# Gate and up products with the tokens held still and the weights streamed; ten of eleven gate chunks from seven Strassen block products

## The chip, the core and the metric

The kernel runs on one core of one Trainium2 chip, as one launch. The metric is the device time of that launch in microseconds (us). Three runs of the kernel before took 1958.15, 1959.32 and 1959.55 us, so its median is 1959.32 us.

## The reference

One decoder block for 256 tokens of width 2048, all in float32:

```
x = layer_norm(2**0.25 * x + 0.5 * swiglu(x, ffn1_w_gate, ffn1_w_up, ffn1_w_down))
x = layer_norm(2**0.25 * x + hybrid_mixer(x))          # attention heads and an RG-LRU branch
x = layer_norm(2**0.25 * x + 0.5 * swiglu(x, ffn2_w_gate, ffn2_w_up, ffn2_w_down))
x = x + sigmoid(x @ w_ple_gate) * (p @ w_ple_proj)

swiglu(x, g, u, d) = (silu(x @ g) * (x @ u)) @ d       # g, u: 2048 x 5632, d: 5632 x 2048
```

The change concerns `swiglu`, which runs twice. Its three weights make up most of what the kernel reads: 528 of the 684 entries of 512 KB belong to them.

## The kernel before

**Numbers in two parts.** TensorE multiplies in a 32-bit format that keeps 12 bits of a factor. So every factor is split in two parts, hi and lo: ScalarE (ACT) writes the rounded hi part (line 86 for weights, line 60 for activations), VectorE (DVE) subtracts it from the original and writes lo (lines 92 and 61). A product is then the sum of three: hi·hi, hi·lo and lo·hi. The tokens are kept transposed in `xT` (16 blocks of 128 input channels, hi and lo).

**The plan.** `make_plan` lists the weights in the order in which the products take them, in entries of 256 rows by 512 columns (512 KB). Each entry is loaded into one of 5 buffers `raw` by SyncE's queue, split into one of 9 slots `hi` and `lo`, and used. `advance` prepares entries up to 7 ahead (`AHEAD`) while a slot is free (`SLOTS`); a slot is free again when the products that read it are done. The order within each engine is the order in which this program writes the instructions.

**The feed-forward stage.** `swiglu` takes the 5632 inner channels in 11 chunks of 512. For each chunk it forms the gate (8 entries) and the up product (8 entries) with `group_a`: a 128x128 block of weights is held in TensorE and the 256 tokens stream past it. For each weight block there are two matmuls: hi of the weights against hi and lo of the tokens (512 columns), and lo of the weights against hi of the tokens (256 columns). The result has the inner channels on the partitions. `evac_a` adds the two halves of a bank (lines 307 and 308), the sigmoid follows (line 412), and the activation is split (lines 60 and 61). Then `down` multiplies the activation of the **previous** chunk by its 8 entries of the third weight, activation held still and weights streamed (three matmuls of 512 columns per block), and adds into `acc` (line 315). So a chunk's activation has two whole products, some 45 us, to become ready before it is used.

**The rest.** The mixer uses `group_a` for 6 groups (`channels`) and `group_b`, which holds tokens still and streams weights, for 5; small pieces of the RG-LRU and the attention are put between entries by `tick`. At the first product after a layer norm (`boundary`) the second half of the tokens is still being transposed, so the products take the two halves of the tokens one after the other.

Of the kernel before, what the change touches and what calls it, by code (L numbers as in the profile page):

```python
# [17 lines left out]
NCH = FF // 512  # L18
QW, KVW, LRU = 1536, 512, 1536
C_X = QW + 2 * KVW  # L20
C_Y = C_X + LRU
HOOKS = (4, 5, 6, 7)
# [9 lines left out]
AHEAD = 7  # L32
SLOTS = 9
# [3 lines left out]
class Block:  # L37
# [26 lines left out]
    def load(self, q):  # L64
        e = self.plan[q]
        if e.get("load"):
            e["load"]()
        e["raw"] = self.tile(self.wraw, [P, 2, 512], F32, "raw")
        for k in e["parts"]:
            self.nc.sync.dma_start(e["raw"][:, k, :], e["src"][:, k, :])  # L70

    def prepare_hi(self, q):
        while self.loaded < min(len(self.plan), q + 4):
            self.load(self.loaded)
            self.loaded += 1
        e = self.plan[q]
        if e.get("split"):
            e["split"]()
        if e["work"]:
            e["hi"], e["lo"] = self.wide_r((P, 2, 512)), self.wide_r((P, 2, 512))  # L80
        else:
            e["hi"] = self.tile(self.whi, [P, 2, 512], F32R, "hi")
            e["lo"] = self.tile(self.wlo, [P, 2, 512], F32R, "lo")
            self.live += 1
        for k in e["parts"]:
            self.nc.scalar.copy(e["hi"][:, k, :], e["raw"][:, k, :])  # L86

    def prepare_lo(self, q):
        e = self.plan[q]
        eng = self.nc.gpsimd if e["pool"] else self.nc.vector  # L90
        for k in e["parts"]:
            eng.tensor_tensor(e["lo"][:, k, :], e["raw"][:, k, :], e["hi"][:, k, :].bitcast(F32), op=ALU.subtract)  # L92
# [9 lines left out]
    def advance_lo(self, end):  # L102
        while self.ready_lo < end:
            self.prepare_lo(self.ready_lo)
            self.ready_lo += 1
# [23 lines left out]
    def tick(self):  # L129
        self.ticks += 1  # L130
        if self.ticks % 2:
            self.tick_lru()
        for queue in (self.att_q, self.gate_q, self.res_q):
            self.step(queue)
# [7 lines left out]
    def make_plan(self):  # L142
        i = self.i
        plan = self.plan = []

        def add(w, r0, c0, n=1, **kw):
            for j in range(n):
                plan.append({"src": self.rows2(w, r0 + 256 * j, c0), "work": False, "pool": False,
                             "parts": [slice(0, 2)], **kw})

        def ffn(name):
            g, u, d = (i[f"{name}_w_{v}"] for v in ("gate", "up", "down"))
            for c in range(NCH):
                add(g, 0, c * 512, 8)
                add(u, 0, c * 512, 8)
                if c:
                    down(d, (c - 1) * 512)
            down(d, (NCH - 1) * 512)

        def down(w, r0):  # L160
            for n in range(4):
                add(w, r0, n * 512, 2)

        w, wo = i["w_in"], i["w_out"]
        ffn("ffn1")
        for j in range(8):
            plan[j]["load"] = lambda j=j: self.load_x(j)
            plan[j]["split"] = lambda j=j: self.split_x(j)
            plan[16 + j]["load"] = lambda j=j: self.load_acc(j)
        plan[0]["parts"] = [slice(0, 1), slice(1, 2)]  # L170
        v0 = len(plan)
        add(w, 0, QW + KVW, 8)
        for g in range(3):
            add(w, 0, C_X + g * 512, 8)
        for h in range(4):
            add(w, 0, h * 512, 8)
        for g in range(3):
            add(w, 0, C_Y + g * 512, 8)
            down(wo, g * 512)
        down(wo, 3 * 512)  # L180
        f0 = len(plan)
        ffn("ffn2")
        p0 = len(plan)
        for n in range(4):
            add(i["w_ple_proj"], 0, n * 512)
        for n in range(4):
            add(i["w_ple_gate"], 0, n * 512, 8)
        for q in (v0, f0, p0):
            for e in plan[q:q + 3]:
                e["work"] = e["pool"] = True  # L190
        plan[p0]["load"], plan[p0]["split"] = self.load_p, self.split_p
        self.xraw = {}
        self.limit = len(plan)
        self.loaded = self.ready = self.ready_lo = self.taken = self.live = 0
        self.ticks = 0
        self.lru_q, self.att_q, self.gate_q, self.res_q = [], [], [], []

    def rows2(self, w, r0, c0):
        return w[r0:r0 + 256, c0:c0 + 512].rearrange("(k p) c -> p k c", p=P)

# [33 lines left out]
    def group_a(self, on_block, boundary=False):  # L234
        banks = [self.bank() for _ in range(4)]
        if not boundary:
            for j in range(8):
                e = self.take()
                self.tokens_a(e, j, banks, slice(0, 256), True, on_block)
                self.done(e)  # L240
                self.tick()
            return
        es = []
        self.limit = self.taken + 8
        for j in range(8):
            es.append(self.take())
            self.tokens_a(es[j], j, banks, slice(0, P), True)
            if j == 1:
                self.advance_lo(self.ready)
            if j in HOOKS:  # L250
                self.ln_transpose(1, HOOKS.index(j))
        self.limit = len(self.plan)
        self.res_q.append(self.ln_residual())
        for j in range(8):
            self.tokens_a(es[j], j, banks, slice(P, 256), False, on_block)
            self.done(es[j])
            self.tick()
# [69 lines left out]

    def down(self, acts, first):
        for n in range(4):
            es = [self.take(), self.take()]  # L330
            for t in range(2):
                self.down_mm(acts, es, t, n, first)
                self.tick()
            for e in es:
                self.done(e)
# [66 lines left out]
    def swiglu(self, boundary):  # L402
        nc = self.nc
        pend = None
        for c in range(NCH):
            gate = []

            def on_gate(b, bank):
                g = self.narrow()
                self.evac_a(bank, g)  # L410
                s = self.narrow()
                nc.scalar.activation(s, g, AF.Sigmoid)  # L412
                nc.vector.tensor_tensor(g, g, s, op=ALU.mult)  # L413
                gate.append(g)

            self.group_a(on_gate, boundary and c == 0)
            if c == 1 and not boundary:
                self.res_q.append(self.tables())
            ah, al = self.wide_r(), self.wide_r()

            def on_up(b, bank):
                u = self.narrow()
                self.evac_a(bank, u)
                nc.vector.scalar_tensor_tensor(u, gate[b], 0.5, u, op0=ALU.mult, op1=ALU.mult)  # L424
                self.split(ah[:, b, :], al[:, b, :], u)

            self.group_a(on_up)
            if pend is not None:
                self.down(pend, c == 1)
            pend = (ah, al)  # L430
        self.down_last(pend)

# [299 lines left out]
    def build(self):  # L732
        tc = self.tc
        with (
            tc.tile_pool(name="const", bufs=1) as self.const,
            tc.tile_pool(name="small", bufs=2) as self.small,
            tc.tile_pool(name="wraw", bufs=5) as self.wraw,
            tc.tile_pool(name="whi", bufs=SLOTS) as self.whi,
            tc.tile_pool(name="wlo", bufs=SLOTS) as self.wlo,
            tc.tile_pool(name="work", bufs=12) as self.work,  # L740
            tc.tile_pool(name="work1", bufs=6) as self.work1,
# [58 lines left out]
```

## Time and profile before

| | |
|---|---|
| median of three runs | 1959.32 us |
| profiled execution, first to last instruction (span) | 1958.6 us |
| TensorE matmuls busy | 1946.0 us, 99% |
| TensorE weight loads busy | 1665.9 us, 85% |
| VectorE busy | 1293.7 us, 66% |
| ScalarE busy | 962.3 us, 49% |
| GpSimd busy | 151.2 us, 8% |
| DMA queue of the weights, share of 16 engines | 58.4% |
| mean DMA rate | 192 GB/s |

The profiled execution is one of the same program; its span stands 0.7 us under the median of the runs. Busy times are unions: a matmul that starts while the one before it drains counts once. So the step from one matmul's start to the next is the time that a matmul takes in a row of them, and not the duration shown beside it, which includes the drain.

### The profile page before, as it was taken

How to read it: one execution, taken by the hardware profiler on the slowest of the kernel's cores; microseconds unless marked ns; L12 is line 12 of the kernel's file. 1: busy time of each engine (PE TensorE's matmuls, PEld its weight loads, DVE VectorE, ACT ScalarE, POOL GpSimd, SP SyncE). 2: the span in 40 equal slices, each digit the busy share in tenths (PEclk: the TensorE clock that was granted, in tenths of full speed). 3: DMA queues.
4: the chain of work that ended last, by engine and by line, in shares of the span. 5: the costliest groups of instructions: out<-in, count | busy, mean ns of one | idle time of the engine just before them, and what ended most of it. 6: DMA issues, size and time to landing. Idle time of an engine off the chain costs nothing.

```text
span 1958.6 us, 26578 instructions
## 1 busy us (share of the span) xinstructions
PE 1946.0 (99%) x10244; PEld 1665.9 (85%) x10244; DVE 1293.7 (66%) x1679; ACT 962.3 (49%) x1330; POOL 151.2 (8%) x93
## 2 busy tenths in 40 slices
PE   8999999999999999999999999999999999999999
PEld 7888888888888888888888898888888888888787
DVE  6667565656665666778677786566556656565875
ACT  6544444444444446656754545444444444444552
POOL 0000000000000012301100250000000000000151
PEclk9999999999999999999999999999999999999999
DMA  9666565556655665655456466656565656655563
GB/s 315 206 210 201 166 218 190 174 171 215 205 176 177 193 205 183 226 163 171 141 193 194 150 207 222 195 172 219 168 214 173 195 169 217 193 173 172 178 223 132
DMA packets 195007, 375.27 MB, mean 192 GB/s; under 512 B 11953, under 2 KB 14657, under 8 KB 194881
## 3 DMA queue, kind: packets, MB, share of 16 engines
q1 hardware_dynamic: 193856, 370.42, 58.4%
q0 software_dynamic: 1024, 3.16, 0.5%
q8 instruction: 80, 1.31, 0.3%
q14 instruction: 47, 0.38, 0.1%
HBM read 371.43 MB, written 2.10 MB: 191 GB/s over the span
## 4 chain that ended last, share of the span: by engine, by line
PE 99%; DVE 1%; DMA 0%; issue 0%; ACT 0%; SPq 0%; POOL 0%; DVEq 0%
PE mm L203 98%; PE mm L380 1%; DVE w L61 0%; DMA raw<-in_ffn_w_gate_dram 0%; DVE lo L92 0%; PE mm L586 0%; DVE bst L358 0%; DVE acc L315 0%; ACT hi L86 0%; POOL rs L367 0%; DVE acc L370 0%; SPq L70 0%; DVE qk L698 0%; PE mm L619 0%; PE mm L618 0%
## 5 line engine op out<-in xcount | busy, mean ns | idle before, releaser
L203 PE MATMUL mm<-xT,hi 128*128 128x512 f32 (+1 forms) x3216 | 1121.3, 393 | 6.2 <-DVE xT L61 5.3
L86 ACT CAST hi<-raw 128x1024 fp32r<-128x1024 f32 (+1 forms) x676 | 693.4, 1048 | 620.7 <-PE mm L203 423.3
L92 DVE TENSOR_TENSOR lo<-raw,hi 128x1024 fp32r<-128x1024 f32 (+1 forms) x676 | 839.5, 1280 | 231.6 <-ACT hi L86 230.1
L203 PE MATMUL mm<-xT,lo 128*128 128x256 f32 (+1 forms) x3216 | 899.1, 280 | 0.0
L203 PEld LDWEIGHTS mm<-xT,hi 128*128 128x128 f32 x3216 | 606.0, 188 | 143.6 <-ACT hi L86 6.4
L203 PEld LDWEIGHTS mm<-xT,lo 128*128 128x128 f32 x3216 | 604.1, 188 | 1.7 <-DVE lo L92 0.8
L203 PE MATMUL mm<-hi,w 128*128 128x512 f32 x1672 | 521.6, 390 | 0.0
L203 PEld LDWEIGHTS mm<-hi,w 128*128 128x128 f32 x1672 | 313.9, 188 | 65.4
L203 PE MATMUL mm<-lo,w 128*128 128x512 f32 x836 | 325.5, 389 | 0.6 <-DVE lo L92 0.6
L308 DVE TENSOR_TENSOR w<-mm,w 128x256 f32<-128x256 f32 x200 | 83.4, 419 | 194.7 <-ACT w L307 194.6
L203 PEld LDWEIGHTS mm<-lo,w 128*128 128x128 f32 x836 | 157.0, 188 | 32.7 <-DVE lo L92 1.0
L203 PE MATMUL mm<-hi,xT 128*128 128x512 f32 (+1 forms) x584 | 180.2, 385 | 0.0
L315 DVE TENSOR_TENSOR acc<-acc,mm 128x512 f32<-128x512 f32 x184 | 122.1, 681 | 63.2 <-PE mm L203 63.2
L92 POOL TENSOR_TENSOR w<-raw,w 128x1024 fp32r<-128x1024 f32 x9 | 25.9, 2911 | 1318.7 <-ACT w L86 679.8
L307 ACT COPY w<-mm 128x256 f32<-128x256 f32 x200 | 72.5, 365 | 112.3 <-PE mm L203 112.3
L203 PEld LDWEIGHTS mm<-hi,xT 128*128 128x128 f32 x584 | 107.2, 188 | 23.1
L203 PE MATMUL mm<-lo,xT 128*128 128x512 f32 (+1 forms) x292 | 111.4, 382 | 0.0
L60 ACT CAST w<-w 128x256 fp32r<-128x256 f32 x90 | 36.5, 407 | 92.3 <-DVE w L424 92.3
L61 DVE TENSOR_TENSOR w<-w,w 128x256 fp32r<-128x256 f32 x90 | 43.2, 481 | 41.9 <-ACT w L60 41.9
L413 DVE TENSOR_TENSOR w<-w,w 128x256 f32<-128x256 f32 x88 | 39.0, 444 | 44.2 <-ACT w L412 44.2
L203 PEld LDWEIGHTS mm<-lo,xT 128*128 128x128 f32 x292 | 54.8, 188 | 11.1
L412 ACT ACTIVATE w<-w 128x256 f32<-128x256 f32 x88 | 36.8, 418 | 48.6 <-DVE w L308 48.5
(125 smaller groups left out, 624.6 us busy)
## 6 DMA issues: line engine op xcount, KB each, us to landing
raw<-in_ffn_w_up_dram SPq DMA_DIRECT2D x176, 512.0 KB, 4.7
raw<-in_ffn_w_down_dram SPq DMA_DIRECT2D x176, 512.0 KB, 4.8
raw<-in_ffn_w_gate_dram SPq DMA_DIRECT2D x175, 512.0 KB, 4.6
raw<-in_w_in_dram SPq DMA_DIRECT2D x88, 512.0 KB, 4.5
raw<-in_w_out_dram SPq DMA_DIRECT2D x32, 512.0 KB, 4.6
raw<-in_w_ple_gate_dram SPq DMA_DIRECT2D x32, 512.0 KB, 4.9
w<-in_ln_g_dram SPq DMA_DIRECT2D x12, 256.0 KB, 9.0
w<-in_ln_b_dram SPq DMA_DIRECT2D x12, 256.0 KB, 7.9
```

What stands on the lines that cost most here:

```text
L60: self.nc.scalar.copy(hi, src)
L61: (self.nc.gpsimd if pool else self.nc.vector).tensor_tensor(lo, src, hi.bitcast(F32), op=ALU.subtract)
L86: self.nc.scalar.copy(e["hi"][:, k, :], e["raw"][:, k, :])
L92: eng.tensor_tensor(e["lo"][:, k, :], e["raw"][:, k, :], e["hi"][:, k, :].bitcast(F32), op=ALU.subtract)
L203: self.nc.tensor.matmul(out, lhsT=lhsT, rhs=rhs, start=start, stop=stop, skip_group_check=True)
L307: self.nc.scalar.copy(c, bank[:, 256:])
L308: self.nc.vector.tensor_tensor(dst, bank[:, :256], c, op=ALU.add)
L315: self.nc.vector.tensor_tensor(a, a, bank, op=ALU.add)
L380: nc.tensor.transpose(bank[:, q * P:(q + 1) * P], self.acc[:, t, kb * P:(kb + 1) * P], self.ident)
L412: nc.scalar.activation(s, g, AF.Sigmoid)
L413: nc.vector.tensor_tensor(g, g, s, op=ALU.mult)
```

## The change

The gate and the up product now hold tokens still and stream weights, as `down` does; the activation then has the tokens on the partitions, and TensorE transposes it (`h_transpose`: 8 transposes for each chunk) before `h_split` splits it for the third product. In chunks 1 to 10 the gate is a product of 2x2 blocks (128 tokens x 1024 channels against 1024 channels x 256 columns) in Strassen's form (Winograd's variant): seven block products, named p1 to p7, with 256 columns in each matmul. The token sums that these need (S1 to S4) are formed and split once per feed-forward stage in `forms`, during chunk 0; the weight differences are formed on VectorE for each chunk, 128x2048 at a time, in the raw buffers (`difference`). The first 512-column chunk keeps an ordinary gate product (`group_b`).

The order within a chunk is now: p5, transposes of the last activation, p2, split of that activation, down 0, p6, down 1, p7, p3, down 2, p4, down 3, up entries 0 to 5, p1 of the next chunk, up entries 6 and 7. In the last chunk down 2 and 3 come after the up product.

Buffers: 6 of 1 MB for raw weights (before 5 of 512 KB), 6 slots hi and lo (before 9), entries prepared 6 ahead (before 7), and 4 small work buffers (before 6). A block of gate weights is loaded in rows of 256 columns, 1 KB each (before 2 KB).

```diff
-AHEAD = 7
-SLOTS = 9
+AHEAD = 6
+SLOTS = 6
+RAWS = 6
...
+    def difference(self, after, out, a, b):
+        if after is not None:
+            self.advance_lo(after["q"] + 1)
+        self.nc.vector.tensor_tensor(out["tile"], a["tile"], b["tile"], op=ALU.subtract)
...
+    def product(self, kind, bank, start):
+        es = []
+        for j in range(2):
+            e = self.take()
+            for k in range(4):
+                self.mm_moving_w(bank[:, :256], self.form(kind, 4 * j + k), e["hi"][:, k, :], e["lo"][:, k, :],
+                                 start and j == 0 and k == 0, j == 1 and k == 3)
+            es.append(e)
+            self.tick()
+        return es
...
+    def gate_first(self):
+        self.X, self.p1 = self.bank(), self.narrow()
+        es = self.product("p1", self.X, True)
+        self.nc.scalar.copy(self.p1, self.X[:, :256])
+        self.finished(es)
+
+    def gate_rest(self, G, h, pend, first, last):
...
+        es = self.product("p5", Z, True)
+        nc.scalar.copy(p5, Z[:, :256])
+        self.finished(es)
+        for t in range(2):
+            self.h_transpose(h, t)
+        es = self.product("p2", X, False)
+        nc.scalar.copy(G[:, 0, :256], X[:, :256])
+        self.finished(es)
+        for t in range(2):
+            self.h_split(pend, t)
+        self.down_one(pend, 0, first)
+        es = self.product("p6", Y, True)
+        nc.vector.tensor_tensor(u2, Y[:, :256], p1, op=ALU.add)
+        self.finished(es)
+        self.down_one(pend, 1, first)
...
+    def up(self, G, next_gate):
+        banks = [self.bank() for _ in range(2)]
+        for j in range(8):
+            if j == 6 and next_gate:
+                self.gate_first()
+            e = self.take()
+            for t in range(2):
+                self.tokens_b(e, j, banks[t], t)
+            if j == 7:
+                for t in range(2):
+                    self.nc.vector.tensor_tensor(G[:, t, :], G[:, t, :], banks[t], op=ALU.mult)
```

How the engines' instructions move is shown at two places. In these rows `raw`, `hi` and `lo` are weights, `w` work buffers and `mm` banks; the second number of a name is that of the tile.

VectorE, first feed-forward stage, ahead of the down stretch that uses chunk 1's activation. Before:

```order
L308 TENSOR_TENSOR w_296_1632<-mm_1434,w_297_1633 128x256
L424 SCALAR_TENSOR_TENSOR w_296_1632<-w_257_1422,w_296_1632 128x256
L61 TENSOR_TENSOR w_261_1430<-w_296_1632,w_260_1429 128x256
L92 TENSOR_TENSOR lo_1592<-raw_1523,hi_1591 128x1024
L92 TENSOR_TENSOR lo_1642<-raw_1545,hi_1641 128x1024
L315 TENSOR_TENSOR acc<-acc,mm_1651 128x512
```

Now, at the same place; `lo_1687` and `lo_1691` belong to p2, `lo_1708` and `lo_1726` to down 0, `lo_1761` and `lo_1768` to p6, `lo_1808` to down 1, line 115 is a difference of weights, line 601 the gate times the up product, line 62 the lo part of the activation:

```order
L109 TENSOR_TENSOR lo_1687<-raw_1505,hi_1686 128x1024
L115 TENSOR_TENSOR raw_1390<-raw_1547,raw_1390 128x2048
L109 TENSOR_TENSOR lo_1691<-raw_1505,hi_1690 128x1024
L601 TENSOR_TENSOR w_185_1153<-w_185_1153,mm_1554 128x512
L601 TENSOR_TENSOR w_185_1153<-w_185_1153,mm_1555 128x512
L109 TENSOR_TENSOR lo_1708<-raw_1572,hi_1707 128x1024
L109 TENSOR_TENSOR lo_1726<-raw_1572,hi_1725 128x1024
L109 TENSOR_TENSOR lo_1761<-raw_1390,hi_1760 128x1024
L115 TENSOR_TENSOR raw_1427<-raw_1547,raw_1427 128x2048
L109 TENSOR_TENSOR lo_1768<-raw_1390,hi_1767 128x1024
L109 TENSOR_TENSOR lo_1808<-raw_1640,hi_1807 128x1024
L62 TENSOR_TENSOR w_281_1731<-mm_1771,w_280_1730 128x4x128
```

The split of the activation stood some 45 us of products ahead of its use in the list; now it stands behind the weights of p6 and of down 1 and two differences, right before the down stretch.

ScalarE at the same place. Before, the activation's hi parts (line 60) and the next weights:

```order
L307 COPY w_297_1633<-mm_1434 128x256
L60 CAST w_260_1429<-w_296_1632 128x256
L86 CAST hi_1641<-raw_1545 128x1024
L86 CAST hi_1647<-raw_1567 128x1024
L86 CAST hi_1681<-raw_1589 128x1024
```

Now, from the copy of p1's result (line 536) to the activation's hi part (line 61); line 545 copies p5's result, line 550 p2's:

```order
L536 COPY w_270_1660<-mm_1659 128x256
L103 CAST hi_1686<-raw_1505 128x1024
L103 CAST hi_1690<-raw_1505 128x1024
L103 CAST hi_1707<-raw_1572 128x1024
L103 CAST hi_1725<-raw_1572 128x1024
L545 COPY w_284_1734<-mm_1733 128x256
L103 CAST hi_1760<-raw_1390 128x1024
L103 CAST hi_1767<-raw_1390 128x1024
L550 COPY w_279_1729<-mm_1659 128x256
L103 CAST hi_1807<-raw_1640 128x1024
L103 CAST hi_1811<-raw_1640 128x1024
L61 CAST w_280_1730<-mm_1771 128x4x128
```

The hi part of p2's first weights now stands behind the copy of p1's result, and that of the activation behind the copy of p2's result and two casts for down 1.

## Rows read from the trace of the kernel before

**Rows 1.** The page: engines' busy time, and the chain that ended last.

```profile
PE 1946.0 (99%) x10244; PEld 1665.9 (85%) x10244; DVE 1293.7 (66%) x1679; ACT 962.3 (49%) x1330; POOL 151.2 (8%) x93
...
PE 99%; DVE 1%; DMA 0%; issue 0%; ACT 0%; SPq 0%; POOL 0%; DVEq 0%
```

**Rows 2.** TensorE's waits: who for whom, us in total, times, longest.

```profile
PE mm L203 <- DVE xT L61: 5.3, 1, 5.3
PE mm L380 <- DVE acc L370: 1.5, 1, 1.5
```

**Rows 3.** TensorE in order of time, second stage: first matmuls of gate, down, gate.

```profile
1227.82 0.40 PE L203 MATMUL mm<-xT,hi 128*128 128x512 f32 x1
...
1272.48 0.39 PE L203 MATMUL mm<-hi,w 128*128 128x512 f32 x1
...
1294.27 0.40 PE L203 MATMUL mm<-xT,hi 128*128 128x512 f32 x1
```

**Rows 4.** TensorE in order of time, last product: tokens held still, 512 and 256 columns.

```profile
1935.00 0.39 PE L203 MATMUL mm<-lo,xT 128*128 128x512 f32 x1
...
1942.70 0.39 PE L203 MATMUL mm<-lo,xT 128*128 128x512 f32 x1
...
1943.29 0.28 PE L203 MATMUL mm<-lo,xT 128*128 128x256 f32 x1
...
1953.83 0.28 PE L203 MATMUL mm<-lo,xT 128*128 128x256 f32 x1
```

**Rows 5.** The chain in order of time: transposes (L380) and the second stage's first gate.

```profile
1107.16 9.19 PE mm L203 x80
1116.36 0.45 PE mm L380 x4
1116.81 1.80 PE mm L203 x16
```

**Rows 6.** VectorE in order of time: down stretch of a chunk; several in a row merged.

```profile
307.02 1.28 DVE L315 TENSOR_TENSOR acc<-acc,mm 128x512 f32<-128x512 f32 x2
...
322.01 4.63 DVE L92 TENSOR_TENSOR lo<-raw,hi 128x1024 fp32r<-128x1024 f32 x4
327.95 1.23 DVE L92 TENSOR_TENSOR lo<-raw,hi 128x1024 fp32r<-128x1024 f32 x1 [1.32 <-ACT hi L86]
```

**Rows 7.** Groups by line and shape: count, busy us, mean ns, idle before.

```profile
L92 DVE TENSOR_TENSOR lo<-raw,hi 128x1024 fp32r<-128x1024 f32 x674 | 838.2, 1282 | 230.1 <-ACT hi L86 228.5 <-PE mm L203 0.9
L86 ACT CAST hi<-raw 128x1024 fp32r<-128x1024 f32 x674 | 692.1, 1050 | 619.1 <-PE mm L203 423.3 <-DMA raw<-in_ffn_w_gate_dram 66.9 <-DMA raw<-in_ffn_w_down_dram 64.1
L307 ACT COPY w<-mm 128x256 f32<-128x256 f32 x200 | 72.5, 365 | 112.3 <-PE mm L203 112.3
L60 ACT CAST xT<-qk 128x512 fp32r<-128x512 f32 x24 | 14.9, 621 | 0.8
L492 DVE SCALAR_TENSOR_TENSOR w<-w 128x12 f32<-128x12 f32 x7 | 1.2, 172 | 0.2
```

**Rows 8.** ScalarE in order of time: three casts of weights in a row.

```profile
1826.31 2.99 ACT L86 CAST w<-raw 128x1024 fp32r<-128x1024 f32 x3
```

**Rows 9.** TensorE in order of time: the start, and after the longest later pause.

```profile
7.32 0.79 PE L203 MATMUL mm<-xT,hi 128*128 128x512 f32 x1 [0.89 <-ACT hi L86]
...
9.07 0.63 PE L203 MATMUL mm<-xT,hi 128*128 128x512 f32 x1
...
9.71 0.63 PE L203 MATMUL mm<-xT,hi 128*128 128x512 f32 x1
...
12.79 0.40 PE L203 MATMUL mm<-xT,hi 128*128 128x512 f32 x1
...
1843.38 0.66 PE L380 MATMUL mm<-ident,acc 128*128 128x128 f32 x4 [1.46 <-DVE acc L370]
...
1844.33 0.63 PE L203 MATMUL mm<-hi,w 128*128 128x512 f32 x2
```

**Rows 10.** DMA issues by line: gate entries, KB each, median us to landing.

```profile
raw<-in_ffn_w_gate_dram SPq DMA_DIRECT2D x175, 512.0 KB, 4.6
```

More of the change, by code (lines that the diff above doesn't have):

```diff
@@ new lines, in entry, with add @@
+        def entry(u, k0, kn, kind):
+            plan.append({"unit": u, "k0": k0, "kn": kn, "need": len(items), "before": [], "work": False, "pool": False,
+                         "parts": [slice(0, kn)], "kind": kind, "q": len(plan)})
+            return plan[-1]
+        def add(w, r0, c0, n=1, kind="b"):
+            for j in range(n):
+                if j % 2 == 0:
+                    m = min(2, n - j)
+                    u = unit([P, 2 * m, 512], m)
+                load(u, 2 * (j % 2), self.rows(w, r0 + 256 * j, 2, c0, 512), 2)
+                entry(u, 2 * (j % 2), 2, kind)
@@ L151, in ffn, with down, block, product @@
+        def down(w, r0, ns=range(4)):
+            for n in ns:
+                add(w, r0, n * 512, 2, "d")
+        def block(w, r0, c0, left):
+            u = unit([P, 8, 256], left)
+            for j in range(2):
+                load(u, 4 * j, self.rows(w, r0 + 512 * j, 4, c0, 256), 4)
+            return u
+        def product(u, kind):
+            return [entry(u, 4 * j, 4, kind) for j in range(2)][1]
         def ffn(name):
             g, u, d = (i[f"{name}_w_{v}"] for v in ("gate", "up", "down"))
+            b11 = p1 = None
@@ new lines, in ffn @@
+                add(u, 0, c0, 6)
+                if c < NCH - 1:
+                    b11 = block(g, 0, c0 + 512, 11)
+                    p1 = product(b11, "p1")
+                    b12 = block(g, 0, c0 + 768, 4)
+                    first_need = len(items)
+                q = len(plan)
+                add(u, 6 * 256, c0, 2)
+                if c < NCH - 1:
+                    plan[q]["before"].append(lambda a=p1, o=b11, x=b12: self.difference(a, o, x, o))
+                else:
+                    down(d, c0 - 512, (2, 3))
@@ L158, in ffn @@
+            q = len(plan)
             down(d, (NCH - 1) * 512)
-        def down(w, r0):
-            for n in range(4):
-                add(w, r0, n * 512, 2)
+            for e in plan[q:q + 2]:
+                e["work"] = True
         w, wo = i["w_in"], i["w_out"]
@@ L232, in tokens_b, with group_a @@
             self.mm_moving_w(bank[:, cols], self.x_act(kb, t), e["hi"][:, k, cols], e["lo"][:, k, cols], kb == 0, kb == KB - 1)
-    def group_a(self, on_block, boundary=False):
+    def group_a(self, on_block):
         banks = [self.bank() for _ in range(4)]
[L236 to L244, printed above, removed]
-        for j in range(8):
[L246 to L256, printed above, removed]
+        for j in range(8):
+            e = self.take()
+            self.tokens_a(e, j, banks, slice(0, 256), True, on_block)
+            self.done(e)
             self.tick()
@@ L402, in swiglu @@
     def swiglu(self, boundary):
-        nc = self.nc
-        pend = None
+        self.sums, self.hT = {}, {}
+        h = None
         for c in range(NCH):
[L406 to L430, printed above, removed]
@@ L431, in swiglu @@
-        self.down_last(pend)
+            last = c == NCH - 1
+            G = self.wide((P, 2, 512))
+            if c == 0:
+                self.group_b(lambda t, bank: self.silu(bank, G, t), boundary)
+                if not boundary:
+                    self.res_q.append(self.tables())
+                self.form_q.append(self.forms())
+            else:
+                act = self.wide_r(), self.wide_r()
+                self.gate_rest(G, h, act, c == 1, last)
+            self.up(G, not last)
```

223 lines of the change are left out of this document (178 added, 45 removed).

## The prediction

> **What bounds the kernel now.** First the busy times and the chain of work that ended last [rows 1]: TensorE is busy for 99% of the span, and 99% of the chain is its matmuls. VectorE is busy for 66% and ScalarE for 49%, so both have room on the average. Then the list of who waited for whom, for TensorE alone [rows 2]: the longest wait is the 5.3 us before the first matmul, the next is 1.5 us. So before the change the time is the sum of TensorE's steps, and the first question is what the change does to them; the second is whether the other engines can still hand over in time. The steps come from TensorE in order of time. In a chunk of the second stage the first down matmul stands at 1272.48 and the gate's first matmuls at 1227.82 and 1294.27 [rows 3]: gate and up take 44.66 us, 22.33 each, down takes 21.79, a chunk 66.45. The last product of the kernel already does what the change does everywhere, tokens still and weights streamed, with three matmuls for each block: with 512 columns eleven such threes take 1942.70 - 1935.00 = 7.70, 0.70 us each; with 256 columns 31 of them take 1953.83 - 1943.29 = 10.54, 0.340 us each [rows 4].
>
> **TensorE's steps after the change.**
> 1. An up product is 32 threes of 512 columns: 22.40 us against 22.33. With the first stage's chunk 0 gate that is 23 x 0.07 = +1.6.
> 2. A Strassen gate is 7 products x 8 threes of 256 columns: 56 x 0.340 = 19.04 against 22.33. Twenty chunks: -65.8. In the old gate a 256-column step takes 0.349 - 0.233 = 0.116 (a pair less a 512-column step) while other engines are busy, against 0.113 at the kernel's end; by that the twenty chunks cost 20 x 168 x 0.003 = 10 more, which I keep as a bound. The order shows the 168 matmuls, so the saving itself is not in doubt.
> 3. The second stage's first gate comes at a boundary. There 16 old matmuls take 1.80 [rows 5], so its 256 take 28.8; the new form streams weights over each token half in any case and takes 22.4: -6.4.
> 4. Eight transposes for each of 22 chunks; four take 0.44 [rows 5]: 22 x 0.88 = +19.4.
>
> Sum: -51.2 us, if TensorE never waits.
>
> **VectorE and ScalarE.** A chunk's VectorE work is now 30 lo parts (24 before), four differences of 128x2048, eight adds into acc, and some ten small adds and products. In a row a lo part costs (4.63 - 1.23)/3 = 1.13 us and an add of a bank 0.60 [rows 6]. No row has a 128x2048 subtraction. Two lo parts in a row, 2.27, are an upper bound; 0.60 for 512 and 1.13 for 1024 elements leave 0.53 for each further 512, which gives 1.13 + 1.06 = 2.19, and I take 2.2. So a chunk needs 34 + 9 + 10 = 53 us of VectorE against 64.1 of TensorE: enough on the average. The average hides one place, and there I expect the loss.
>
> **The wait at down 0.** The two order listings of the change show it. ScalarE casts p2's first weights only behind the copy of p1's result, and VectorE has twelve instructions from p2's first lo part to the lo part of the activation without which down 0 cannot pass its third matmul. From p1's last matmul on TensorE has: up entries 6 and 7 (eight threes, 5.60), p5 (2.72), transposes (0.88), p2 (2.72) and two matmuls of down (0.45): 12.37 us. The other side: the matmul's drain 0.17 (0.28 less a step of 0.11 [rows 4]), the copy 0.37 and the cast 1.05 [rows 7], then seven lo parts 7.9, two differences 4.4, two products with the up banks 1.2 and the activation's lo part 0.68: 15.8 us. TensorE waits 3.4 us. ScalarE by itself gives nearly the same: after p2 drain 0.17, copy 0.37, two casts 2.0 (three take 2.99 [rows 8]) and the activation's hi part 0.62 [rows 7] make 3.16 us to the first matmul. So 3.2 is the lower bound even if VectorE were free. The upper bound takes each operation by itself and not in a row: lo 1.28 [rows 7], difference 2.56, 512 columns 0.68, in all 17.7, a wait of 5.3. I take 3.5, a tenth above the sum for the handovers: 20 x 3.5 = +70. It comes back in every chunk, since the count starts anew at each p1: during up entries 0 to 5 VectorE needs 1.13 in each 2.8 and catches up.
>
> Behind this place the same count finds nothing late. After down 0, VectorE does an add, a difference and a lo part in 0.60 + 2.2 + 1.13 = 3.9, and TensorE needs that lo part after p6, half a down product and one step, 2.72 + 1.40 + 0.23 = 4.35. p7, p3, p4 and down 1 to 3 then have their parts 0.5 to 3 us ahead.
>
> **Chunk 0.** `forms` puts twelve operations of 1024 elements on VectorE, and in the first stage the tables stand there too, some 28 tiny operations of 0.172 [rows 7]. Up to the split of S1, which p5 needs, VectorE has nine lo parts 10.2, two differences 4.4, nine form operations at 1.15 10.4, two products of the sigmoid 1.3, and the tables 4.9: 31.2 against 25.1 of TensorE. p5 waits 6.1; the remaining three splits then make the wait at down 0 6.4 and not 3.5: +9 in all. In the second stage, without tables, +4. Sum +13, bounds 0 (the work is spread over slack that I don't see) and 20.
>
> **The rest.** At each stage's end the activation's lo part stands behind the last down's add: 0.17 + 0.60 + 0.69 less two matmuls, 1 us, twice: +2. In the mixer five entries are ready ahead and not seven; at 2.8 us an entry that still covers 14 us of small work, so I cost it at nothing; without that cover a few us. The gate's loads are hidden: each block of weights is asked for over 10 us before use, an entry lands in 4.6 [rows 10], and twice as many packets of half the size, were each as long as a whole one, would raise the DMA share from 58 to some 75%.
>
> Sum: -51.2 + 70 + 13 + 2 = +34. The profiled span is 1958.6 and the runs' median 0.7 above it, so 1993 on that scale; I say 1994.
>
> **Rivals.**
> - *The wait is hidden, TensorE stays the bound* (the other side). What would have to be so: the twelve operations and what is ahead of them take under 12.4 us. For it: VectorE has a fifth of its time free. Against it: none of the twelve can start before p1's result is copied, and ScalarE's route alone gives 3.2. Time: 1959.3 - 51.2 + 4 = 1912. It decides from a wait of 2.4 us downwards, where waits and saving cancel.
> - *The clock falls in the pauses.* At the start of the kernel a pair of matmuls takes 9.71 - 9.07 = 0.64 and the first of it 0.63; from 12.79 on it is 0.40 [rows 9], and a pair takes 0.349. That is the lower of the two levels (1.2 and 2.4 GHz), after 7 us in which the engine had hardly begun. These 5 us from 7.32 on cost 5.5 x (1 - 0.349/0.64) = some 2.5. After the longest later pause, 1.46 us before 1843.38, the steps are at full speed again at once [rows 9]. The new pause is twice that long, so the trace leaves it open: 20 x 2.5 = 50 more, 2044. The Trainium skill, "TensorE: Matmul & The Clock Gate", section "HAM oscillation — how this bites in real kernels", says just this of pauses for data that come back in each turn of a loop: the clock gate closes in them, and each turn begins at the lower clock. By that rule the time would be this rival's 2044; by the row at 1843.38 it is 1994. The pause here is broken by two matmuls, and I follow the row.
> - *Single durations hold and not those in a row*: wait 5.3, 20 x 1.8 = 36 more: 2030. It has the same cause as the forecast and only another size.
>
> **Chances.** The forecast with its sizes: 0.66, with a range of its own from 1972 (ScalarE's bound, nothing in chunk 0) to 2040 (single durations, the 10 us of step 2). The clock: 0.12, around 2044. The wait hidden in whole or in most: 0.22, from 1912 up to no change. The range that leaves out no more than two in ten is 1952 to 2050. Measurement can tell 0.2%, 3.9 us, from no change: faster by more 0.18, within 0.04, slower 0.78.
>
> **What would show it.** In the new trace TensorE should wait for line 62 (the activation's lo part) and line 61 some 3 to 4 us in each of 20 chunks, 70 us in all, and be busy for about 96%; the longest waits stand at chunk 1 of each stage, before p5 and at down 0. A Strassen product's 24 matmuls should take 2.72 us, an up entry 2.80, a chunk about 67.6. VectorE should show four subtractions of 128x2048 near 2.3 us each and be busy near 80%. If the first matmuls behind each pause are 0.43 and not 0.23 apart, it is the clock. I am wrong if TensorE hardly waits at line 62, since then the saving of 51 us stays, or if a chunk's steps differ from 64.1 without waits.

## The result, and the profile after

The changed kernel takes 2098.24 us (median of 4 runs, 2096.43 to 2101.1), the kernel before 1958.74 (1958.04 to 1959.55): 1.0711 times as long, 95% interval 1.0696 to 1.0727. The forecast was 1994, range 1952 to 2050. The direction was right, but the loss is 139.5 us and not 34.

The page of the changed kernel; first the busy times, then the chain of work that ended last.

```profile
PE 1979.3 (94%) x10324; PEld 1683.0 (80%) x10324; DVE 1574.5 (75%) x1695; ACT 1043.8 (50%) x1254; POOL 160.9 (8%) x93
...
PE 11%; issue 1%; DVE 0%; POOL 0%; ACT 0%; POOLq 0%; DVEq 0%
```

TensorE is busy for 94% (99% before, [rows 1]). Its busy time is longer, 1979.3 against 1946.0 us, though the plan had less work for it: its steps became slower too. The chain breaks off after some 12% of the span here, so it says nothing of the rest, and the waits have to be read directly.

TensorE's waits in the changed kernel: who for whom, us in total, times, longest.

```profile
PE mm L299 <- ACT w L61: 57.3, 21, 2.8
PE mm L299 <- DVE w L62: 22.4, 11, 9.9
PE mm L299 <- DVE lo L109: 18.2, 6, 10.3
...
PE mm L299 <- ACT w L786: 1.5, 1, 1.5
PE mm L299 <- ACT qk L820: 1.4, 1, 1.4
PE mm L785 <- DVE qk L779: 1.2, 2, 0.9
```

Where there had been one long wait [rows 2], there are 20 of 2.8 us and one of 0.5 for the high part of the activation (L61), shorter ones for its low part and two of 9.9 and 6.9 us for those of sums (all L62), one of 10.3 us for a weight's low part (L109), and three new ones in the mixer (L786, L820, L779).

TensorE in order of time, one chunk of the second stage and the start of the next: first up matmul, end of p2, down 0, first up matmul.

```profile
1303.02 0.40 PE L299 MATMUL mm<-hi,xT 128*128 128x512 f32 x1
...
1334.61 0.28 PE L299 MATMUL mm<-hi,xT 128*128 128x256 f32 x1
1337.72 0.50 PE L299 MATMUL mm<-hi,w 128*128 128x512 f32 x1 [2.84 <-ACT w L61]
1338.05 0.40 PE L299 MATMUL mm<-lo,w 128*128 128x512 f32 x1
1339.01 0.74 PE L299 MATMUL mm<-hi,w 128*128 128x512 f32 x2 [0.56 <-DVE w L62]
...
1340.95 1.06 PE L299 MATMUL mm<-hi,w 128*128 128x512 f32 x2
1341.80 0.63 PE L299 MATMUL mm<-lo,w 128*128 128x512 f32 x1
1342.23 1.06 PE L299 MATMUL mm<-hi,w 128*128 128x512 f32 x2
...
1373.66 0.40 PE L299 MATMUL mm<-hi,xT 128*128 128x512 f32 x1
```

The chunk takes 1373.66 - 1303.02 = 70.64 us (66.45 before, [rows 3]); from transposes to transposes the chunks take 69.94 to 71.84, 70.83 on the mean of 18. The pause stands where it was forecast, but from 1340 on three matmuls take 1342.23 - 1340.95 = 1.28 us, 0.43 each, where three take 0.68 elsewhere. That is the sign which the prediction gave for the clock.

The same stretch in windows, ahead of it one of the first stage's start, and behind it two of a later chunk whose down 0 begins at 1549.06. Each row has the us, then busy time and count of TensorE, its weight loads, VectorE, ScalarE and GpSimd, then granted clock, DMA share, GB/s.

```profile
60.00:70.00 10.00, 4.29 (x15) 3.60 (x16) 9.59 (x20) 3.67 (x7) 0.00 (x0) 0.50 0.00 1
...
1337.70:1339.00 1.30, 0.73 (x2) 0.30 (x2) 1.30 (x3) 0.46 (x1) 0.00 (x0) 1.00 0.03 11
...
1340.00:1343.00 3.00, 3.00 (x8) 2.36 (x8) 0.10 (x1) 0.00 (x0) 0.00 (x0) 0.50 0.00 0
...
1344.00:1350.00 6.00, 6.00 (x39) 5.43 (x38) 4.02 (x4) 4.21 (x4) 0.00 (x0) 1.00 0.01 2
...
1548.30:1549.00 0.70, 0.00 (x0) 0.00 (x0) 0.70 (x2) 0.70 (x3) 0.00 (x0) 0.50 0.02 9
1549.00:1555.00 6.00, 5.94 (x13) 4.32 (x14) 1.87 (x4) 0.49 (x2) 0.00 (x0) 0.50 0.00 0
```

In the first of the two chunks the granted clock falls to 0.50, the lower of the two levels (1.2 and 2.4 GHz), 2.3 us after the engine has begun to work again (with a second gap of 0.56 us in between); by 1344 it is back. In the second it stands at 0.50 while TensorE still waits, and stays there through 6 us of work. Of the 20 pauses at down 0, 14 are like the second (the clock falls in the last 0.9 us of the pause or as it ends) and 6 like the first (0.7 to 2.3 us behind it); the low stretch lasts 3.4 us in ten of them and 6.8 in the other ten. At the start of the first stage, where TensorE waits for VectorE (9.59 of 10 us busy), it stands at 0.50 all through the window. Over the whole profile its mean is 0.966.

With the first transposes of the layer norm behind each stage as marks, the span's 138.5 us lie so: first stage +75.9, mixer +6.9, second stage +55.7, the end 0. Ten steady chunks of +4.19 us make 41.9 in each stage, which leaves 34.0 in the rest of the first stage and 13.8 in the rest of the second (with the mean of the chunks in the place of the one shown, 3 and 1 us less). In the first stage's chunk 0, VectorE in order of time shows one cause:

```profile
55.32 0.17 DVE L682 TENSOR_SCALAR w<-par 128x12 f32<-128x12 f32 x1 [11.22 <-DMA par<-in_par_dram]
```

VectorE stands still for 11.2 us in front of a tiny operation of the tables, whose parameters have not landed. SyncE's queue, in order of time, shows that their transfer was issued last, behind eleven loads of weights, only at 47.52:

```profile
31.70 4.19 SPq L77 DMA_DIRECT2D raw<-in_ffn_w_gate_dram  x3
...
43.99 3.49 SPq L77 DMA_DIRECT2D raw<-in_ffn_w_down_dram  x2
47.52 0.66 SPq L646 DMA_DIRECT2D par<-in_par_dram  x1
```

### The profile page after: what moved, and what is told of

Same layout as the page of the kernel before. It is cut to its first block, busy times and chain, and to the rows that moved or that the text cites. A ratio compares the mean times of both kernels' runs of the same rounds, so it can differ in the third digit from the quotient of the medians.

```text
span 2097.1 us, 26430 instructions
## 1 busy us (share of the span) xinstructions
PE 1979.3 (94%) x10324; PEld 1683.0 (80%) x10324; DVE 1574.5 (75%) x1695; ACT 1043.8 (50%) x1254; POOL 160.9 (8%) x93
## 3 DMA queue, kind: packets, MB, share of 16 engines
q0 software_dynamic: 1024, 3.16, 0.5%
## 5 line engine op out<-in xcount | busy, mean ns | idle before, releaser
L109 DVE TENSOR_TENSOR lo<-raw,hi 128x1024 fp32r<-128x1024 f32 (+1 forms) x786 | 968.9, 1263 | 232.4 <-ACT hi L103 231.0
L299 PE MATMUL mm<-hi,w 128*128 128x512 f32 (+1 forms) x2904 | 786.3, 358 | 78.3 <-ACT w L61 57.3
L299 PE MATMUL mm<-hi,xT 128*128 128x512 f32 (+1 forms) x3016 | 832.5, 360 | 6.3 <-ACT hi L103 6.3
L299 PEld LDWEIGHTS mm<-hi,w 128*128 128x128 f32 x2904 | 526.7, 198 | 164.9 <-ACT w L61 61.7
L299 PEld LDWEIGHTS mm<-hi,xT 128*128 128x128 f32 x3016 | 538.5, 190 | 97.4 <-ACT hi L103 7.0
L299 PE MATMUL mm<-lo,xT 128*128 128x512 f32 (+1 forms) x1508 | 542.5, 360 | 18.2 <-DVE lo L109 18.2
L299 PE MATMUL mm<-lo,w 128*128 128x512 f32 (+1 forms) x1452 | 516.5, 356 | 0.0
L299 PEld LDWEIGHTS mm<-lo,xT 128*128 128x128 f32 x1508 | 287.0, 190 | 66.6 <-DVE lo L109 21.4
L115 DVE TENSOR_TENSOR raw<-raw,raw 128x2048 f32<-128x2048 f32 x80 | 183.9, 2299 | 0.7
L109 POOL TENSOR_TENSOR w<-raw,w 128x1024 fp32r<-128x1024 f32 x9 | 26.5, 2957 | 1535.8 <-ACT w L103 1535.8
L299 PEld LDWEIGHTS mm<-xT,hi 128*128 128x128 f32 x384 | 72.2, 188 | 16.9
L299 PEld LDWEIGHTS mm<-xT,lo 128*128 128x128 f32 x384 | 72.1, 188 | 0.3
```

The costliest lines, as they stand in the source:

```text
L109: eng.tensor_tensor(e["lo"][:, k, :], self.raw(e)[:, k, :], e["hi"][:, k, :].bitcast(F32), op=ALU.subtract)
L115: self.nc.vector.tensor_tensor(out["tile"], a["tile"], b["tile"], op=ALU.subtract)
L299: self.nc.tensor.matmul(out, lhsT=lhsT, rhs=rhs, start=start, stop=stop, skip_group_check=True)
```

## The experiments

The median of the kernel before stood between 1958.9 and 1959.9 in these comparisons. My theory was that three things add up: the pause at down 0 with low clock behind it, waits in chunks 0 and 1 for what is set up there, and a queue in the mixer that the six slots make. The rival: VectorE, with all its added work, falls behind everywhere, and whatever is moved, the wait turns up in another place.

**1. The activation split early.** The split of the activation moves from behind p2 to right behind the transposes, ahead of p2, and both now stand before p5's slots are given back.

```diff
         es = self.product("p5", Z, True)
         nc.scalar.copy(p5, Z[:, :256])
-        self.finished(es)
         for t in range(2):
             self.h_transpose(h, t)
+        for t in range(2):
+            self.h_split(pend, t)
+        self.finished(es)
         es = self.product("p2", X, False)
...
-        for t in range(2):
-            self.h_split(pend, t)
         self.down_one(pend, 0, first)
```

> The activation's transposes are followed at once by its split (lines 61 and 62), ahead of the casts and differences for p6 and down 1; all else as in the changed kernel. Theory A (the pause at down 0 is the place in the list, and the low clock behind it is its consequence): TensorE no longer waits at down 0, the granted clock stays 1.00 in the chunks, each of 20 chunks loses its pause of 3.0 to 3.8 us and 1.8 to 2.4 us of low clock, so 2097 - 20 x 5.4 = about 1990. Rival B (VectorE has too much to do as a whole, and the pause only shows where it is late): the wait moves to p6 or down 1 and the time stays above 2060.

Measured: 1992.62 us (1991.62 to 1994.3), 1.0168 times before [1.0153, 1.0184], 105.6 us under the changed kernel. TensorE's transposes of two steady chunks, in order of time:

```profile
1338.39 1.04 PE L584 MATMUL mm<-ident,w 128*128 128x128 f32 x8
...
1403.86 1.03 PE L584 MATMUL mm<-ident,w 128*128 128x128 f32 x8
```

The chunk's period is 1403.86 - 1338.39 = 65.47 us, so the pause with all that follows it cost 70.64 - 65.47 = 5.17 us. It is the place of the split in ScalarE's and VectorE's order that makes it, not the amount of work.

**2. The pause filled.** Nothing is moved, but between p2 and down 0 TensorE does 24 matmuls into a bank that nobody reads.

```diff
+        fill = self.bank()
+        for _ in range(24):
+            self.mm(fill[:, :256], self.xT[:, 0, 0, :P], self.xT[:, 0, 0, :], True, True)
         self.down_one(pend, 0, first)
```

> Between p2 and down 0, 24 matmuls of 256 columns on a spare bank that nobody reads (2.8 us) keep TensorE at work during the pause; waits and order of the other engines stay. Theory A (down 0 is slow because the clock falls in the pause): the pause stays in the account, but down 0 runs at full speed, 1.8 to 2.4 us less in each of 20 chunks, so about 2055. Rival B (down 0 is slow for another reason, such as a late bank or contention): the time stays at 2097 or rises.

Measured: 2063.2 us (2061.53 to 2063.97), 1.0527 [1.0511, 1.0542]: extra work made the kernel 35.0 us faster. TensorE in order of time, with the transposes (L587 here) of this chunk and the next, and one row of its list of waits:

```profile
1310.90 1.04 PE L587 MATMUL mm<-ident,w 128*128 128x128 f32 x8
...
1314.51 3.02 PE L299 MATMUL mm<-xT 128*128 128x256 f32 x24
1317.51 0.50 PE L299 MATMUL mm<-hi,w 128*128 128x512 f32 x1
...
1379.93 1.04 PE L587 MATMUL mm<-ident,w 128*128 128x128 f32 x8
...
PE mm L299 <- DVE w L62: 29.1, 24, 9.9
```

Down 0 starts no earlier than it did (3.0 us behind p2's last step), and the windows behind it show a granted clock of 1.00:

```profile
1318.00:1324.00 6.00, 5.44 (x25) 4.30 (x24) 2.03 (x4) 1.05 (x1) 0.00 (x0) 1.00 0.00 1
```

So 35.0/20 = 1.75 us of each chunk's 5.17 are the clock, and 3.42 the pause. This kernel's own chunk, 1379.93 - 1310.90 = 69.03 us, gives 69.03 - 65.47 = 3.56 for the pause and 70.83 - 69.03 = 1.80 for the clock on the mean. The waits for L62 rose from 11 to 24: with the clock up, TensorE waits some 0.5 us more for the activation's low part in each of the 20 chunks.

**3. The tables during chunk 2.** Their generator is queued at chunk 2 and not at chunk 0.

```diff
-                if not boundary:
-                    self.res_q.append(self.tables())
...
+                if c == 2 and not boundary:
+                    self.res_q.append(self.tables())
```

> The tables (rotary angles, decay) are formed during chunk 2 of the first stage, and no longer beside the token sums in chunk 0. Theory A (chunk 0 of the first stage loses its time to VectorE standing before the parameters' transfer, 11.2 us, and to the tables' small operations, 5 us): 14 to 22 us less, about 2078. Rival B (the token sums alone make chunk 0 late): under 6 us less.

Measured: 2085.87 us (2083.7 to 2087.09), 12.4 under the changed kernel, a little less than expected. The first transposes in the changed kernel, then in this one, and VectorE's first operation on the parameters here:

```profile
88.05 1.03 PE L584 MATMUL mm<-ident,w 128*128 128x128 f32 x8
...
68.14 1.03 PE L584 MATMUL mm<-ident,w 128*128 128x128 f32 x8
...
139.84 0.17 DVE L682 TENSOR_SCALAR w<-par 128x12 f32<-128x12 f32 x1
```

Chunk 0 is 19.9 us shorter. At chunk 2 the parameters have landed in time (no wait stands behind that row), but the chunk takes 77.60 us and not 71.24, which leaves these 6.4 us to the tables' own operations.

**4. The kernel before with six slots.** Nothing of Strassen, only the slots and the lead of the changed kernel, and the few entries that it prepares in work buffers.

```diff
-AHEAD = 7
-SLOTS = 9
+AHEAD = 6
+SLOTS = 6
```

> The kernel before with 6 slots and entries 6 ahead, and the same entries in work buffers as in the changed kernel, nothing else. Theory A (fewer slots make ScalarE wait for TensorE in its list, and small pieces of the mixer behind it come late): about 7 us in the mixer, 1966. Rival B (the mixer's 7 us come from the larger transfers or the smaller work pool): 1959, within 2 us.

Measured: 1968.35 us (1966.67 to 1970.3), 1.0043 [1.0029, 1.0057]. TensorE's waits in this kernel:

```profile
PE mm L212 <- ACT w L596: 1.5, 1, 1.5
PE mm L212 <- ACT qk L630: 1.5, 1, 1.5
...
PE mm L595 <- DVE qk L589: 1.2, 2, 0.9
```

These are the changed kernel's three waits in the mixer, to a tenth, and by the marks used above the mixer takes 7.0 us more than before (6.9 in the changed kernel). So six slots with six entries ahead bring it, without the larger transfers and the smaller pool of work buffers; slots and lead were not tried one without the other.

**5 to 7. What is left, taken apart.** The sixth run puts the early split and the tables (during chunk 3) together. The fifth also gives chunk 1 an ordinary gate, with the transposes and the split after its fourth entry, so that the sums are formed during chunk 1. The seventh gives every chunk that ordinary gate. In the fifth, `gate_plain` takes the eight entries with the split among them, queues the forms, and does down 0 to 3; in the seventh no forms are needed.

```diff
+            elif c == 1:
+                act = self.wide_r(), self.wide_r()
+                self.gate_plain(G, h, act)
...
-            if c == 0:
+            if c == 1:
                 self.finish(self.form_q)
```

> The early split of the first experiment, and besides it chunk 1's gate is ordinary too (so Strassen runs in chunks 2 to 10), the token sums are formed during chunk 1 and the parameters' tables during chunk 3. Theory A: what the early split left over (33 us above the kernel before) sits in chunks 0 and 1 and in the mixer, not in the Strassen chunks, whose period of 65.47 us is below the 66.45 us of before. Then 18 x -0.98 = -17.6 us, two ordinary chunks with transposes +2, the stage ends +2, the mixer +7: about 1953 us, under the kernel before. Theory B: the forms and tables cost the same wherever they stand, since VectorE is the engine that falls behind: the waits move to chunks 1 to 3 and the time stays at 1985 us or above.

> The early split, and the tables during chunk 3, nothing else. Theory A: the transfer of the parameters behind the weights' loads holds VectorE's queue 11.2 us whatever is split early, so as much comes back as in the run with the tables alone (12.4 us): 1980 us. Theory B: the early split had already taken what that stall cost, under 4 us are left: 1989 us or above.

> No Strassen products at all: every gate chunk is eight block products with the tokens stationary, as the chunk 0 of the changed kernel, with the transposes, the early split and the late tables. Theory A: the Strassen form does save TensorE time, about 2 us in a chunk (an ordinary chunk with its transposes costs 66.45 + 1.0 = 67.5 us against 65.47): about 1959 + 22 + 7 = 1988 us, some 35 us above the run with the forms in chunk 1. Theory B: at the products' measured step of 0.117 to 0.120 us the form saves nothing, and this kernel comes within 8 us of that run.

Measured: split and tables 1978.38 us (1977.29 to 1979.36), 1.0095 [1.008, 1.011]; with the forms in chunk 1 1953.8 us (1951.15 to 1954.17), 0.9964 [0.995, 0.9978]; all ordinary 1986.36 us (1985.25 to 1988.52), 1.0137 [1.0122, 1.0153]. All three fell where the first theory put them, within 2 us. The busy times of the kernel with the forms in chunk 1, from its page:

```profile
PE 1926.2 (99%) x10180; PEld 1640.7 (84%) x10180; DVE 1531.9 (78%) x1665; ACT 1033.7 (53%) x1236; POOL 156.4 (8%) x93
```

This is the version that beats both kernels, by 0.36% the one before and by 6.9% the changed one. Against the kernel with ordinary gates, Strassen with its sums is worth 1986.36 - 1953.8 = 32.6 us in 18 chunks, 1.8 us each: little more than half of the 22.33 - 19.04 = 3.29 that the steps of the forecast gave.

**8. GpSimd's work in the second stage.** The products and additions of the layer norms' residual (24 of each in the three layer norms, and not 32 in all as the expectation says) are left out of the kernel of the early split.

```diff
-                nc.gpsimd.tensor_tensor(a, a, gb[:, 0, :], op=ALU.mult)
-                nc.gpsimd.tensor_tensor(a, a, gb[:, 1, :], op=ALU.add)
                 yield
```

> The kernel of the early split without GpSimd's 32 products and additions of the layer norms' residual (the residual's scale and shift are left out; their transfers stay). Theory A: while GpSimd does these, VectorE's operations take up to twice as long, and that is what makes the sums late in the second stage's chunk 0 (a wait of 9.9 us and others): VectorE's operations there go back to 1.2 us for 128x1024, the wait falls under 4 us, and the time falls by 6 to 14 us to about 1982. Theory B: the slow VectorE operations there have another cause, such as the transfers: they stay slow, and the time is within 2 us of 1992.6.

Measured: 1978.51 us (1977.45 to 1979.4), 14.1 under the kernel of the early split. The second stage starts only 1.4 us earlier and takes 13.4 us less by the marks used above, so nearly all of it lies there. VectorE in order of time with the residual, GpSimd beside it, and TensorE's wait for the first sum:

```profile
1163.96 2.16 POOL L481 TENSOR_TENSOR acc<-acc,w 128x512 f32<-128x512 f32 x1
...
1164.89 1.27 DVE L579 SCALAR_TENSOR_TENSOR w<-mm,qk 128x512 f32<-128x512 f32 x2
...
1167.22 2.31 DVE L492 TENSOR_TENSOR w<-xT 128x1024 f32<-128x1024 f32 x1
...
1202.25 0.79 PE L299 MATMUL mm<-hi,w 128*128 128x256 f32 x2 [9.90 <-DVE w L62]
```

and without it:

```profile
1163.78 1.22 DVE L489 TENSOR_TENSOR w<-xT 128x1024 f32<-128x1024 f32 x1
...
1188.00 0.50 PE L299 MATMUL mm<-hi,w 128*128 128x256 f32 x2 [2.82 <-DVE w L62]
```

The operation takes 1.22 us and not 2.31. The wait for the sums in the second stage fell from 9.9 to 2.8 us, under the expected 4. Low clock goes with it: of the 17 us at 0.50 in the second stage's first two chunks, none are left. The longest wait for a sum in this kernel, 6.9 us, is that of the first stage, where GpSimd does nothing.

**9 to 11. The step of 256 columns by itself.** Behind the end of the kernel of the early split stand matmuls that serve nothing, each row of them with one pair of operands (`x` a slice of xT, `w` a slice of a weight's high part in a work buffer; `st` is held still, `mv` moves).

```diff
+        for n, (st, mv) in enumerate(((x, x), (w, x), (x, w), (w, w))):
+            for _ in range(24):
+                self.mm(b[0][:, :256], st[:, :P], mv[:, :256], True, True)
```

> The kernel of the early split with matmuls of 256 columns behind its end, for the step alone: 24 with xT stationary and xT moving, 24 with a work buffer stationary, 24 with a work buffer moving, 24 with both (that buffer is a slice of a weight's high part), all with no other engine at work, then 80 while VectorE makes four subtractions of 128x2048, then 240 in which four transfers of 1 MB land. Theory A: the step of 0.117 to 0.120 us in the Strassen products comes of the other engines' traffic: alone it is 0.113 us or less whatever buffer is read, and 0.117 or more beside the subtractions or the transfers. Theory B: it comes of the buffer that the stationary operand is read from: alone already 0.117 with xT and 0.120 with a work buffer, and the subtractions and the transfers change nothing. The kernel's own time tells nothing here.

> The step alone again, behind the end of the same kernel, now with the pair of operands that had the short step in quiet (a slice of a weight's high part stationary, xT moving: 0.1133 us): 48 in quiet, then 400 in a row, beside which VectorE makes four subtractions of 128x2048, then ScalarE four copies of 128x2048, then four transfers of 1 MB land, then nothing. Theory A: traffic lengthens the step where it is short: 0.113 in quiet and at the end, 0.117 to 0.120 beside one of the three. Theory B: the step goes by the two operands' places alone: 0.113 all through. The kernel's own time tells nothing here.

> Behind the end of the kernel of the early split, with no other engine at work: four products as Strassen's first two kinds (24 matmuls of 256 columns: a slice of xT stationary, high, low, high part of a weight's entry moving) in the four quarters of xT, and a fifth with a slice of a work buffer stationary, as the products with sums. In the steady chunk the three matmuls took 0.352 us with xT and 0.360 with sums, the last product of the kernel before 0.340. Theory A: it is the operands' places: here too 0.352 and 0.360 for the three. Theory B: it is what the rest of the kernel does beside a product: here 0.340 for both. The kernel's own time tells nothing here.

TensorE in the first of the three, in order of time; the name of the moving operand stands first, one name means both:

```profile
1986.17 3.02 PE L299 MATMUL mm<-xT 128*128 128x256 f32 x24
1989.04 2.88 PE L299 MATMUL mm<-xT,w 128*128 128x256 f32 x24
1991.76 2.99 PE L299 MATMUL mm<-w,xT 128*128 128x256 f32 x24
1994.59 3.04 PE L299 MATMUL mm<-w 128*128 128x256 f32 x24
1997.46 38.55 PE L299 MATMUL mm<-xT 128*128 128x256 f32 x320
```

From start to start by 24, the steps are 0.1196 (both in xT), 0.1133 (work buffer still, xT moving), 0.1179 (the reverse) and 0.1196 (both in work buffers); the 320 beside VectorE's subtractions and the transfers 0.120. In the second of the three the short pair, beside VectorE, ScalarE and transfers of some 350 GB/s in turn:

```profile
1985.91 50.94 PE L299 MATMUL mm<-xT,w 128*128 128x256 f32 x448
```

(50.94 - 0.28)/447 = 0.1133: none of the three lengthens it. In the third, four products with xT still, and then one with a work buffer still:

```profile
1986.51 0.28 PE L299 MATMUL mm<-hi,xT 128*128 128x256 f32 x1
...
1997.39 0.28 PE L299 MATMUL mm<-hi,w 128*128 128x256 f32 x1
...
2000.15 0.28 PE L299 MATMUL mm<-hi,w 128*128 128x256 f32 x1
```

With xT the 96 steps take 10.88 us, 0.340 for three; with the work buffer 23 take 2.76, 0.360 for three, as in the steady chunk. So the longer step of the four products with sums belongs to where the operands lie, with the other engines still as well; the work buffer held a weight's part here in the place of a sum. The 0.352 of the three products with xT in the steady chunk is not explained by it: alone they have 0.340, and no kind of traffic that was tried lengthened a short step.

## Why the prediction was wrong

Step by step, the forecast against what was measured, in us:

| term | forecast | measured |
|---|---|---|
| steps of 20 Strassen chunks, transposes in them | 20 x (64.1 - 66.45) = -47 | 20 x (65.47 - 66.45) = -19.6 |
| pause at down 0 | +70 | 20 x 3.42 = +68 |
| clock in these pauses | 0 | +35 |
| rest of the first stage | +11 | +34.0 |
| rest of the second stage | 0 | +13.8 |
| mixer | 0 | +6.9 |
| sum | +34 | +138 |

- **Right: the pause.** Its place, its cause (ScalarE's and VectorE's order ahead of the activation's split) and its size held, 3.4 to 3.6 us against 3.5. With the clock up, both engines' counts show: ScalarE's part first, then 0.5 us more for VectorE's, in each chunk of run 2. In 14 of the changed kernel's 20 pauses the second wait does not show; in the chunk at 1549.06 the matmuls ahead of it run at the lower clock. A 128x2048 subtraction takes 2.30 us (2.2 taken).
- **Wrong: the rejection of the clock rival.** It held, with some 1.8 us a pause and not 2.5. I followed the row at 1843.38 [rows 9], a pause of 1.46 us behind which the steps are at full speed. It does not speak for a pause of 3.0, and the step itself said that the trace left this open; then 0.12 was too little, and the 35 us belonged in the likeliest case. The stated range held the clock's 2044, but only with every other term as forecast. My reason was that the pause is broken by two matmuls; these come behind 2.84 us of it, and in 14 of 20 pauses the clock has fallen by then. The rule that the prediction weighed, in the Trainium skill, "TensorE: Matmul & The Clock Gate", section "HAM oscillation — how this bites in real kernels", agrees with what runs 1 and 2 show: a pause that returns in each turn of the loop is paid a second time in low clock, here some 1.8 us behind 3.4 to 3.6.
- **Wrong: the term of Strassen's saving.** A product was to take 2.72 us and takes 2.82 to 2.91 with xT and 2.87 with sums, the chunk 65.47 without its pause and not 64.1. Of these 1.37 us the seven products' steps make 0.93 (19.97 against 19.04 in the chunk shown for run 1); most of the rest is down 1, which takes 5.91 us there where the other three take 5.47, a delay that the early split brings. The 0.340 of the three [rows 4] came from the end of the kernel and from xT held still; four of the seven products hold sums in work buffers, whose step is 0.120 (run 11). The bound that I kept, 10 us for twenty chunks, was about half of the 20 x 0.93 = 19 that the steps cost, and the whole term is off by 20 x 1.37 = 27.
- **Wrong: the term of chunk 0.** +13 was forecast with a bound of 20, and the rests of the two stages came to 37 us more than their forecast. In the first stage the tables were counted as 28 tiny operations on VectorE. What they cost on top is VectorE's stop for their parameters, whose transfer the change moves behind eleven loads in SyncE's queue. Chunk 0 is 19.9 us shorter without the tables, and some 6 of these come back where they then stand, so 12.4 us are gained in run 3, and 14.2 between runs 1 and 6. The order of SyncE's queue could have been read beforehand. In the second stage GpSimd's residual nearly doubles VectorE's operations (run 8, 14.1 us, low clock included), and between the pauses of the first stage's chunk 0 the clock is low as well (0.50 in the window shown).
- **Wrong, and small: the mixer at nothing.** Six slots and the shorter lead cost the kernel before 8.6 us, 7.0 of them in the mixer (run 4), where I had counted only entries that lie ready. That the mixer's small pieces queue on ScalarE behind a cast which waits for a slot is my reading of the order, and no run shows it by itself.

The doubling by GpSimd stood in the trace of before, in a row that I did not read. VectorE there, in order of time, at the start of the second stage, with one row of GpSimd between:

```profile
1127.87 3.49 DVE L92 TENSOR_TENSOR lo<-raw,hi 128x1024 fp32r<-128x1024 f32 x3
...
1136.75 1.28 POOL L397 TENSOR_TENSOR acc<-acc,w 128x512 f32<-128x512 f32 x1 [25.68 <-DMA w<-in_ln_g_dram]
...
1143.91 17.95 DVE L92 TENSOR_TENSOR lo<-raw,hi 128x1024 fp32r<-128x1024 f32 x8
```

Three low parts take 3.49 us ahead of GpSimd's work, which begins at 1136.75; eight take 17.95, 2.24 each, while GpSimd works. The step went by the mean of the group and by a stretch in the middle of a stage [rows 6, 7], though the forms stand at its start.

Open remains why three matmuls with xT take 0.352 us in the chunk and 0.340 alone, (0.352 - 0.340) x 8 x 3 products x 20 chunks = some 6 us, and what it is in the places of two operands that makes a step long or short.

## What to carry over

A wait that a change brings into every turn of a loop can cost twice, once as a pause and once as the clock behind it (here 3.4 to 3.6 us and 1.8). Filling it with idle matmuls separates the two, and moving the awaited operation up in its engine's queue removes both. Durations for a new operation are read from the place in the program where it will stand, with what the other engines do there, and not from the group's mean or the quiet end. Work that is set up once (tables, sums) is queued where its engine has slack: here moving it, with one ordinary chunk more, turned +1.7% into -0.4%.

## What the runs showed of the hardware

- Behind each of the 20 pauses of 2.84 us at down 0 the granted clock stood at 0.50 for 3.4 or 6.8 us and came back under full work. It fell between 0.9 us before the work began again and 2.3 us after. 24 matmuls into an unread bank kept it at 1.00. Shorter pauses, ahead of the transposes of a layer norm: after 1.2 to 1.5 us it stayed at 1.00 in every trace of this case, and at the last layer norm's 2.0 to 2.1 us it fell in 7 of 12 traces.
- The step of a 256-column matmul differs with the buffers in which its two operands lie, from 0.1133 us (run 10) to 0.120 (run 11) with the other engines still. VectorE, ScalarE and transfers of some 350 GB/s did not change it for the pair tried (run 10).
- VectorE's operations of 128x1024 with two operands in SBUF take 2.3 us and not 1.2 while GpSimd works through tensors of its own; those of 128x512 with one operand in PSUM (L579) keep their 0.6 each (1.27 for two in run 1, 1.29 for two without the residual). The Trainium skill, "SBUF — State Buffer", section "Who interferes with whom", says that these two engines share an interface, which a VectorE instruction with two inputs in SBUF needs and one of them holds for a whole instruction. The rows agree.
